# The seven products of an FFN block in another order, with the fourth sum of the weights multiplied last

## The chip, the cores and the metric

The kernel runs on one core of a Trainium2 chip. The metric is the device time of one execution in microseconds (us). The engines are TensorE (PE; PEld is its loading of weights), VectorE (DVE), ScalarE (ACT), GpSimd (POOL) and the sync engine (SP), which issues most DMAs.

## The reference

Two layers of a block with attention, Fourier mixing and a Hyena convolution run over x (512 tokens x 1024) and a context (256 x 1024); each ends with a feed-forward part (FFN). The change is in x's FFN:

```python
def dwconv3(u, w, b):
    up = jnp.pad(u, ((0, 0), (1, 1), (0, 0)))
    return up[:, :-2] * w[0] + up[:, 1:-1] * w[1] + up[:, 2:] * w[2] + b

def conv_ffn(h, w_up, w_c, b_c, w_down):
    u = dwconv3(h @ w_up, w_c, b_c)
    gate, val = jnp.split(u, 2, axis=-1)
    return (jax.nn.silu(gate) * val) @ w_down
```

The hidden width is 2816, so `w_up` is 1024 x 5632 and `w_down` 2816 x 1024. All is float32.

## The kernel before

**Products.** TensorE multiplies float32 values in a reduced form, so every operand is split into a high and a low part and each product is three matmuls: `mm3` does high x high (L196), weight-high x other-low (L197) and weight-low x other-high (L198). `split` makes the parts: ScalarE casts the high part (L181), and VectorE, or GpSimd where it is told so, subtracts it from the source for the low part (L182).

**x's FFN (`ffn_x`).** The hidden width is cut into 22 blocks m of 128 gate and 128 value columns. The up projection of a block, which would be eight products of quarter matrices, is done in the manner of Strassen and Winograd with seven. x's side is cut into quarters by token half and by input half, with sums of quarters S1 to S4 made once. The weights' side is made per block: `prep(m)` loads the raw weights r[0] (gate) and r[1] (value) on the sync queue (L1269, tag "Wm", three buffers), splits r[0] into the quarters "11" and "21", and lets POOL make four differences of quarters: t13 (L1276, L1277) and t24 (L1278, L1279). Each half of t13 gives a factor T1, T3, each half of t24 a factor T2, T4; the "fourth sum" is the second half of t24. The sums' tag "L" has three buffers for two tiles a block. `later()` splits t24, t13 and the second half of r[1] (w22, the quarter "22"), into buffers of the tags "Wh" and "Wl" (four each). In the profile t13 and t24 are both `tt`, their parts `Wh` and `Wl`, w22's parts `w`.

A product is twelve matmuls of a 128 x 128 weight tile with 256 tokens. `first(m)` does 11·11 into the PSUM tile a (copied by ScalarE, L1298) and 12·21 into c (added by VectorE, L1300). `rest(m)` does the other five, in the order 22·T4, S1·T1, S2·T2, S4·22, S3·T3, with a second PSUM tile b; a product with `False` accumulates on what the tile holds. ScalarE copies and VectorE adds collect the results in C0 (gate) and C1 (value). Then the convolution over tokens (L636 to L638, ScalarE and VectorE), silu (ScalarE, L1334), the product gate x value (POOL, L1335) and the split of the result, gT. For blocks after the first, `rest(m)` calls `prep(m + 1)` and `later()` just ahead of the convolution. For block 0, several first products run ahead while norm and modulation are still under way.

**Down projection (`ffn_down`).** Blocks are taken in pairs; the pair before is multiplied with `w_down` (1024 wide, split in the same way) once the present pair's first block is done, and added to y (L1202). So gT is used some two blocks after it is made.

**What sets the order.** The program yields after each product, and a scheduler with a timeline of its own places all instructions: each engine then runs its list strictly in order, and other blocks' products, the down projection's matmuls and the next layer's modulation (for instance the gate's add, L326, which waits for a DMA of `rows`) may come between. PSUM tiles `pn` come from four, `pw` from two buffers.

Of the kernel before, what the change touches and what calls it, by code (L numbers as in the profile page):

```python
# [12 lines left out]
ALU = mybir.AluOpType  # L13
# [55 lines left out]
class Net:  # L69
# [1171 lines left out]
    def ffn_x(self, l):  # L1241

        nc, st = self.nc, self.X
# [9 lines left out]
        def half(a, i):  # L1253
            return a[:, i * 512 : (i + 1) * 512]

        def quad(a, i):
            return a[:, i * 512 : (i + 1) * 512].rearrange("p (k c) -> p k c", c=P)
# [8 lines left out]
        def prep(m):  # L1266
            r = [self.tl([P, 1024], F32, "Wr" if m == 0 else "Wm", "r") for _ in range(2)]
            for e in range(2):
                nc.sync.dma_start(r[e], self.I["w_up"][l, m, e].rearrange("p k c -> p (k c)"))  # L1269
            q = lambda x, i: tuple(quad(a, i) for a in x)  # L1270
            if m not in w:
                h = self.tl([P, 1024], F32R, "Wh"), self.tl([P, 1024], F32R, "Wl")
                self.split(*h, r[0], E0[m] if m < 2 else None)
                w[m] = {"11": q(h, 0), "21": q(h, 1)}
            t13, t24 = (self.tl([P, 1024], F32, "L", "tt") for _ in range(2))
            te.tensor_tensor(half(t13, 0), half(r[1], 0), half(r[0], 0), op=ALU.subtract)  # L1276
            te.tensor_tensor(half(t13, 1), half(r[1], 1), half(r[1], 0), op=ALU.subtract)  # L1277
            te.tensor_tensor(half(t24, 0), half(r[1], 1), half(t13, 0), op=ALU.subtract)  # L1278
            te.tensor_tensor(half(t24, 1), half(t24, 0), half(r[0], 1), op=ALU.subtract)  # L1279

            def later():
                h = [(self.tl([P, 1024], F32R, "Wh"), self.tl([P, 1024], F32R, "Wl")) for _ in range(2)]
                f = self.M("w22")
                with self.tc.issue_after(self.hi) if 0 < m < 3 else self.tc.issue_after(self.mod) if PIN and m == 0 else nullcontext():
                    el = E1[m] if m < 2 else None
                    self.split(*h[1], t24, el)
                    self.split(*h[0], t13, el)
                    self.split(half(f, 0), half(f, 1), half(r[1], 1), el)
                w[m].update({"T1": q(h[0], 0), "T3": q(h[0], 1), "T2": q(h[1], 0), "T4": q(h[1], 1), "22": (quad(f, 0), quad(f, 1))})

            u["w", m] = later
# [11 lines left out]
        def prod(m, ps, left, right, start=True):  # L1303
            for k in range(4):
                wh, wl = w[m][right]
                sh, sl = S[left]
                self.mm3(ps, (wh[:, k], wl[:, k]), (sh[:, k], sl[:, k]), start and k == 0, k == 3, skip_group_check=True)
            yield 12 * C256, 0.0

        def rest(m):  # L1310
            a, C0 = u.pop(m)
            C1 = self.T(512, "C", tag=Z["CT"][2])
            C = C0, C1
            b = self.pn()[:, :256]
            yield from prod(m, b, "22", "T4")
            nc.scalar.copy(C0[:, 256:512], b)
            b = self.pn()[:, :256]
            yield from prod(m, b, "S1", "T1")
            nc.scalar.copy(C1[:, 256:512], b)
            yield from prod(m, a, "S2", "T2", False)  # L1320
            nc.scalar.copy(C1[:, 0:256], a)
            yield from prod(m, b, "S4", "22", False)
            nc.vector.tensor_tensor(C1[:, 0:256], C1[:, 0:256], b, op=ALU.add)
            yield from prod(m, a, "S3", "T3", False)
            nc.vector.tensor_tensor(C0[:, 256:512], a, C0[:, 256:512], op=ALU.subtract)  # L1325
            nc.vector.tensor_tensor(C1[:, 256:512], a, C1[:, 256:512], op=ALU.add)
            if 2 <= m + 1 < MF:
                prep(m + 1)
                u.pop(("w", m + 1))()
            o = [self.T(512, "ft") for _ in range(2)]  # L1330
            for i in range(2):
                self.ffn_conv(l, m, i, o[i], C[i])
            gt = self.M("gT").rearrange("p (e t) -> p e t", e=2)
            nc.scalar.activation(o[0], o[0], AF.Silu)  # L1334
            nc.gpsimd.tensor_tensor(o[0], o[0], o[1], op=ALU.mult)  # L1335
            self.split(gt[:, 0], gt[:, 1], o[0])
            g[m] = gt

        groups = [list(range(a, a + G)) for a in range(0, MF - 4, G)] + [list(range(MF - 4, MF))]
        for i, ms in enumerate(groups):  # L1340
            for j, m in enumerate(ms):
                if m == 0:
                    pw = [self.pw() for _ in range(2)]
                    for n in range(NF[l]):
                        if n < 4:
                            u["a", n] = pw[n % 2][:, n // 2 * 512 : n // 2 * 512 + 512]
                        (prep if n < 2 else prep_first)(n)
                        yield from first(n)
                    if l:
                        self.need("norm_xf3")  # L1350
                    for n in range(2):
                        u.pop(("w", n))()
                    if l == 0 and Z["RC"] == -1:
                        yield from self.rest_c
                    yield from rest(0)
                    if l == 0 and Z["RC"] == 0:
                        yield from self.rest_c
                    continue
                if m >= NF[l]:
                    yield from first(m)  # L1360
                if l == 0 and Z["RC"] == m + 0.5:
                    yield from self.rest_c
                yield from rest(m)
                if l == 0 and Z["RC"] == m:
                    yield from self.rest_c
                if i and j == 0:
                    yield from self.ffn_down(l, st, g, groups[i - 1], i == 1)
# [334 lines left out]
```

## Time and profile before

| | us |
|---|---|
| median of three runs | 1788.12 (1787.71 to 1790.4) |
| profiled execution | 1784.91 |
| its span | 1783.1 |
| TensorE busy | 1639.1 (92%) |
| VectorE busy | 1440.1 (81%) |
| ScalarE busy | 934.9 (52%) |
| GpSimd busy | 692.3 (39%) |

Times within the profile count from the start of the span. x's FFN of layer 0 lies at about 700 to 1070, that of layer 1 at about 1390 to 1765. A row of a timeline gives the start, the duration, the engine, the line, the instruction with out<-in by the program's names, and in brackets how long the engine stood idle ahead of it and which instruction ended that. A row with x2 holds two like instructions in succession.

### The profile page before, as it was taken

To read this page: it belongs to the slowest core of one execution; us is meant where nothing else is said; L and a number is where in the kernel's file an instruction comes from. 1 tells how busy PE (TensorE), PEld (TensorE's weight loads), DVE (VectorE), ACT (ScalarE), POOL (GpSimd) and SP (SyncE) were. 2 spreads that over 40 slices of the span, in tenths; PEclk is the share of its full clock that TensorE was granted. 3 is DMA by queue.
4 is the path that set the end of the run, shared out by engine and by line. 5 is a ranking of instruction groups with operands and counts; after the bars stand their busy time and mean duration, and the time that the engine had idled before them with its cause. 6 is when DMAs were issued, how large, how long until landed. Compare 5 with 4: busy or idle time off the path is not lost. (4 is left out here: it accounts for less than half of the span.)

```text
span 1783.1 us, 27842 instructions
## 1 busy us (share of the span) xinstructions
PE 1639.1 (92%) x10502; PEld 1397.4 (78%) x10502; DVE 1440.1 (81%) x2324; ACT 934.9 (52%) x1737; POOL 692.3 (39%) x515
## 2 busy tenths in 40 slices
PE   5799987899999997989999998998898799999997
PEld 2677775687788897878989885787787678889996
DVE  5888777697665688889988987668895878999997
ACT  2642344487565454556554556434773465555454
POOL 3343332000134337665554645212002455655543
PEclk9899999999999998999999999999999899999999
DMA  9214277603477642332342258653012343332323
GB/s 366 101 61 146 86 243 263 232 13 130 162 253 232 228 155 71 96 118 84 101 148 84 89 185 305 213 175 118 1 48 83 130 146 103 95 107 86 127 62 119
DMA packets 70003, 248.01 MB, mean 139 GB/s; under 512 B 8111, under 2 KB 9647, under 8 KB 69868
## 3 DMA queue, kind: packets, MB, share of 16 engines
q1 hardware_dynamic: 60716, 215.54, 35.6%
q0 software_dynamic: 9152, 30.68, 5.5%
q8 instruction: 83, 1.36, 0.3%
q14 instruction: 52, 0.43, 0.1%
HBM read 232.03 MB, written 14.16 MB: 138 GB/s over the span
## 5 line engine op out<-in xcount | busy, mean ns | idle before, releaser
L196 PE MATMUL pn<-h,Wh 128*128 128x256 f32 x1328 | 376.6, 286 | 11.7 <-DVE ft L638 4.3
L198 PE MATMUL pn<-h,Wl 128*128 128x256 f32 x1328 | 372.8, 284 | 10.2 <-DVE Wl L182 10.2
L197 PE MATMUL pn<-h,Wh 128*128 128x256 f32 x1328 | 374.2, 283 | 1.7 <-POOL h L182 1.7
L196 PEld LDWEIGHTS pn<-h,Wh 128*128 128x128 f32 x1328 | 253.2, 191 | 24.5 <-issue 7.8
L198 PEld LDWEIGHTS pn<-h,Wl 128*128 128x128 f32 x1328 | 252.1, 191 | 15.3 <-DVE Wl L182 12.7
L197 PEld LDWEIGHTS pn<-h,Wh 128*128 128x128 f32 x1328 | 253.8, 191 | 6.2 <-POOL h L182 2.4
L181 ACT CAST Wh<-Wr 128x1024 fp32r<-128x1024 f32 x118 | 122.7, 1049 | 138.9 <-PE pw L198 46.4
L182 DVE TENSOR_TENSOR Wl<-Wr,Wh 128x1024 fp32r<-128x1024 f32 x89 | 129.7, 1465 | 53.7 <-ACT Wh L181 53.2
L1276 POOL TENSOR_TENSOR tt<-r,r 128x512 f32<-128x512 f32 x44 | 75.0, 1705 | 233.9 <-DMA r<-w_up 211.0
L196 PE MATMUL pw<-Wh,gT 128*128 128x512 f32 x352 | 137.5, 404 | 9.0 <-ACT gT L181 3.9
L197 PE MATMUL pw<-Wl,gT 128*128 128x512 f32 x352 | 138.5, 396 | 3.1 <-DVE Wl L182 3.1
L198 PE MATMUL pw<-Wh,gT 128*128 128x512 f32 x352 | 137.8, 396 | 1.8 <-DVE gT L182 1.8
L181 ACT CAST Wh<-tt 128x1024 fp32r<-128x1024 f32 x88 | 90.8, 1048 | 84.9 <-PE pn L197 42.4
L182 DVE TENSOR_TENSOR Wl<-tt,Wh 128x1024 fp32r<-128x1024 f32 x88 | 122.5, 1411 | 11.0 <-ACT Wh L181 8.0
L1335 POOL TENSOR_TENSOR ft<-ft,ft 128x512 f32<-128x512 f32 x44 | 70.8, 1609 | 132.4 <-DVE ft L638 94.2
L1202 DVE TENSOR_TENSOR y<-y,pw 128x1024 f32<-128x1024 f32 x82 | 99.2, 1213 | 20.1 <-PE pw L198 20.0
L182 POOL TENSOR_TENSOR h<-tf,h 128x256 fp32r<-128x256 f32 (+1 forms) x40 | 36.0, 921 | 187.8 <-ACT h L181 186.5
L182 POOL TENSOR_TENSOR Wl<-Wr,Wh 128x1024 fp32r<-128x1024 f32 x29 | 74.6, 2578 | 57.7 <-ACT Wh L181 56.5
L1278 POOL TENSOR_TENSOR tt<-r,tt 128x512 f32<-128x512 f32 x44 | 75.8, 1722 | 51.9 <-DVE Wl L182 51.9
L196 PE MATMUL pw<-h,Wh 128*128 128x256 f32 (+1 forms) x224 | 76.9, 343 | 13.9 <-DVE v L638 2.6
L283 PE MATMUL pn<-wm,cpad 128*32 128x256 f32 x768 | 67.6, 411 | 19.7 <-DMA wm<-w_mod 19.3
L636 ACT ACTIVATE ft<-C,vec 128x512 f32<-128x512 f32 x88 | 68.7, 811 | 32.1 <-DVE C L1325 25.7
(361 smaller groups left out, 4706.1 us busy)
## 6 DMA issues: line engine op xcount, KB each, us to landing
wm<-w_mod SPq DMA_DIRECT2D x96, 512.0 KB, 5.4
r<-w_up SPq DMA_DIRECT2D x90, 512.0 KB, 3.6
Wr<-w_down SPq DMA_DIRECT2D x66, 512.0 KB, 3.8
L<-w_up SPq DMA_DIRECT2D x44, 512.0 KB, 4.4
Wr<-w_out SPq DMA_DIRECT2D x24, 512.0 KB, 3.6
Wr<-w_in_t SPq DMA_DIRECT2D x16, 512.0 KB, 3.9
dft<-hdft_x POOLq DMA_DIRECT2D x16, 512.0 KB, 4.1
Wr<-w_in_c SPq DMA_DIRECT2D x12, 512.0 KB, 3.6
```

What stands on the lines that cost most here:

```text
L181: r = nc.scalar.copy(hi, src)
L182: (el or nc.vector).tensor_tensor(lo, src, f32(hi), op=ALU.subtract)
L196: nc.tensor.matmul(ps, l[0], r[0], start=first, stop=False, **kw)
L197: nc.tensor.matmul(ps, l[0], r[1], start=False, stop=False, **kw)
L198: nc.tensor.matmul(ps, l[1], r[0], start=False, stop=last, **kw)
L283: nc.tensor.matmul(ps[32 * g : 32 * g + 32, cs], self.cpad[:, q % 2 * 4 + g, :], w[:, g, :], start=q % 2 == 0, stop=q % 2 == 1, skip_group ...
L636: nc.scalar.activation(dst, ps, AF.Identity, scale=w1, bias=b)
L1202: nc.vector.tensor_tensor(y, y, acc[t], op=ALU.add)
L1276: te.tensor_tensor(half(t13, 0), half(r[1], 0), half(r[0], 0), op=ALU.subtract)
L1278: te.tensor_tensor(half(t24, 0), half(r[1], 1), half(t13, 0), op=ALU.subtract)
L1335: nc.gpsimd.tensor_tensor(o[0], o[0], o[1], op=ALU.mult)
```

## The change

In `later()` t24 is split last in place of first. In `rest(m)` the five products come in the order S1·T1, S4·22, S2·T2, S3·T3, 22·T4. Before, 22·T4 was copied to C0's second half and subtracted from a at the end; now a is copied there by ScalarE and 22·T4, in a PSUM tile of its own, is subtracted by VectorE as the last step. The number of instructions of each kind is the same: three copies by ScalarE and three adds by VectorE a block.

```diff
                     el = E1[m] if m < 2 else None
-                    self.split(*h[1], t24, el)
                     self.split(*h[0], t13, el)
                     self.split(half(f, 0), half(f, 1), half(r[1], 1), el)
+                    self.split(*h[1], t24, el)
...
             b = self.pn()[:, :256]
-            yield from prod(m, b, "22", "T4")
-            nc.scalar.copy(C0[:, 256:512], b)
-            b = self.pn()[:, :256]
             yield from prod(m, b, "S1", "T1")
             nc.scalar.copy(C1[:, 256:512], b)
+            yield from prod(m, b, "S4", "22", False)
             yield from prod(m, a, "S2", "T2", False)
             nc.scalar.copy(C1[:, 0:256], a)
-            yield from prod(m, b, "S4", "22", False)
             nc.vector.tensor_tensor(C1[:, 0:256], C1[:, 0:256], b, op=ALU.add)
             yield from prod(m, a, "S3", "T3", False)
-            nc.vector.tensor_tensor(C0[:, 256:512], a, C0[:, 256:512], op=ALU.subtract)
+            nc.scalar.copy(C0[:, 256:512], a)
             nc.vector.tensor_tensor(C1[:, 256:512], a, C1[:, 256:512], op=ALU.add)
+            b = self.pn()[:, :256]
+            yield from prod(m, b, "22", "T4")
+            nc.vector.tensor_tensor(C0[:, 256:512], C0[:, 256:512], b, op=ALU.subtract)
```

The new lines of `rest` have the numbers L1316 (copy of S1·T1), L1319 (copy of a after S2·T2), L1320 (add of b), L1322 (copy of a after S3·T3), L1323 (add of a) and L1326 (subtraction of 22·T4).

First, VectorE at the start of layer 0's FFN, as the difference of the two orders. `tt_7139` and `tt_7140` are t13 and t24 of block 0, `tt_7181` and `tt_7182` those of block 1.

```order
+L182 TENSOR_TENSOR Wl_7216<-tt_7139,Wh_7215 128x1024
 L1300 TENSOR_TENSOR C_7145<-C_7145,pn_7146 128x256
 L182 TENSOR_TENSOR Wl_7218<-tt_7140,Wh_7217 128x1024
-L182 TENSOR_TENSOR Wl_7216<-tt_7139,Wh_7215 128x1024
+L182 TENSOR_TENSOR Wl_7227<-tt_7181,Wh_7226 128x1024
 L182 TENSOR_TENSOR gc_7011<-ft_7056,gc_7011 128x256
 L1300 TENSOR_TENSOR C_7187<-C_7187,pn_7188 128x256
 L182 TENSOR_TENSOR Wl_7229<-tt_7182,Wh_7228 128x1024
-L182 TENSOR_TENSOR Wl_7227<-tt_7181,Wh_7226 128x1024
```

The low part of t13 of block 0 moves ahead of block 0's add of 12·21, and that of block 1 ahead of block 1's; ScalarE's casts move in the same way.

Second, VectorE in layer 1 around the gate's add, L326, before. `tt2836` and `tt2837` are t13 and t24 of block 4, `w222842` is its w22, `Wl2857` the low part of block 5's raw gate weights.

```order
L182 TENSOR_TENSOR Wl2835_14907<-r2832_14902,Wh2834_14906 128x1024
L637 SCALAR_TENSOR_TENSOR ft2844_14928<-C2827_14825,vec1_101,ft2844_14928 128x511
L638 SCALAR_TENSOR_TENSOR ft2844_14928<-C2827_14825,vec1_101,ft2844_14928 128x511
L326 TENSOR_TENSOR G2752_14366<-pn2850_14970,bb2849_14968 128x512
L182 TENSOR_TENSOR Wl2841_14919<-tt2837_14911,Wh2840_14918 128x1024
L182 TENSOR_TENSOR Wl2839_14917<-tt2836_14910,Wh2838_14916 128x1024
L182 TENSOR_TENSOR w222842_14920<-r2833_14903,w222842_14920 128x512
L182 TENSOR_TENSOR gT2845_14935<-ft2843_14927,gT2845_14935 128x512
L182 TENSOR_TENSOR Wl2857_15049<-r2854_15044,Wh2856_15048 128x1024
```

And the same place now:

```order
L182 TENSOR_TENSOR Wl2839_14917<-tt2836_14910,Wh2838_14916 128x1024
L637 SCALAR_TENSOR_TENSOR ft2843_14927<-C2738_14304,vec1_101,ft2843_14927 128x511
L637 SCALAR_TENSOR_TENSOR ft2844_14928<-C2827_14825,vec1_101,ft2844_14928 128x511
L638 SCALAR_TENSOR_TENSOR ft2843_14927<-C2738_14304,vec1_101,ft2843_14927 128x511
L638 SCALAR_TENSOR_TENSOR ft2844_14928<-C2827_14825,vec1_101,ft2844_14928 128x511
L1300 TENSOR_TENSOR C2846_14940<-C2846_14940,pn2848_14942 128x256
L326 TENSOR_TENSOR G2752_14366<-pn2850_14970,bb2849_14968 128x512
L182 TENSOR_TENSOR Wl2841_14919<-tt2837_14911,Wh2840_14918 128x1024
L182 TENSOR_TENSOR Wl2857_15049<-r2854_15044,Wh2856_15048 128x1024
L182 TENSOR_TENSOR w222842_14920<-r2833_14903,w222842_14920 128x512
L182 TENSOR_TENSOR gT2845_14935<-ft2843_14927,gT2845_14935 128x512
```

t13's low part has moved ahead of L326, and block 5's first weights ahead of w22 and gT.

Third, TensorE in a block of layer 1's steady part, before. `h2740` and `h2741` are the high and low part of x's quarter 22, `h2743` and `h2744` of S1, `h2745` and `h2746` of S2; `Wh3040` holds T1 and T3, `Wh3042` T2 and T4; `pn3049` is a.

```order
L196 MATMUL pn3052_16336<-h2740_14318,Wh3042_16284 128x256
L197 MATMUL pn3052_16336<-h2741_14319,Wh3042_16284 128x256
L198 MATMUL pn3052_16336<-h2740_14318,Wl3043_16285 128x256
L196 MATMUL pn3053_16350<-h2743_14325,Wh3040_16282 128x256
L197 MATMUL pn3053_16350<-h2744_14326,Wh3040_16282 128x256
L196 MATMUL pn3049_16307<-h2745_14330,Wh3042_16284 128x256
```

And now:

```order
L198 MATMUL pn3052_16336<-h2743_14325,Wl3041_16283 128x256
L196 MATMUL pn3053_16390<-h2740_14318,Wh3042_16284 128x256
L197 MATMUL pn3053_16390<-h2741_14319,Wh3042_16284 128x256
L196 MATMUL pn3049_16307<-h2745_14330,Wh3042_16284 128x256
L197 MATMUL pn3049_16307<-h2746_14331,Wh3042_16284 128x256
L198 MATMUL pn3049_16307<-h2745_14330,Wl3043_16285 128x256
```

Before, the block's five products begin with all of 22·T4, then two matmuls of S1·T1, then S2·T2. Now they begin with S1·T1; two matmuls of 22·T4 and then S2·T2 follow, and the other ten of 22·T4 stand behind S2·T2, ahead of S4·22 and S3·T3.

## Prediction

> **What bounds the kernel now.** I read the page's first part, then the table of windows over the two stretches in which x's feed-forward part runs, then TensorE's timeline for the waits inside them, and last the engines that those waits name. The profiled execution took 1784.91 us (span 1783.1); the median of the three runs is 1788.12, 3.2 more, and I carry that difference along unchanged. About 0.2%, 3.6 us, is what a measurement of this kernel can tell from no change.
>
> The first line is the page's busy line; the others are windows (length, then busy time of PE, PEld, DVE, ACT, POOL, the granted clock, the DMA share and GB/s).
>
> ```profile
> PE 1639.1 (92%) x10502; PEld 1397.4 (78%) x10502; DVE 1440.1 (81%) x2324; ACT 934.9 (52%) x1737; POOL 692.3 (39%) x515
> 700.00:910.00 210.00, 193.95 (x1300) 177.95 (x1299) 183.74 (x230) 117.81 (x189) 121.45 (x72) 0.96 0.34 110
> 910.00:1060.00 150.00, 146.43 (x1020) 135.20 (x1020) 134.38 (x150) 78.25 (x123) 77.09 (x50) 1.00 0.34 110
> 1395.00:1492.00 97.00, 81.65 (x582) 71.08 (x581) 79.72 (x94) 49.43 (x79) 56.35 (x36) 0.93 0.40 132
> 1492.00:1755.00 263.00, 259.49 (x1784) 239.16 (x1784) 243.60 (x271) 139.11 (x216) 129.48 (x78) 1.00 0.32 102
> ```
>
> TensorE sets the pace. In the steady part of layer 1 it is busy for 259.49 of 263 us and in layer 0 for 146.43 of 150: 3.5 us in each is all that any order of work could win there, and the number of products is unchanged. In the ramps, where the first blocks' weights are still being made, it is idle for 16 of 210 and 15 of 97 us. VectorE is next: 243.60 of 263 is 93%, so in the steady part it has little to give. A gain has to come from the ramps and a loss would come through VectorE.
>
> These are TensorE's waits in the ramps that the change can reach (start, duration, instruction, and in brackets the idle time ahead of it with its releaser):
>
> ```profile
> 722.85 0.39 PE L196 MATMUL pn<-h,Wh 128*128 128x256 f32 x1 [0.31 <-ACT Wh L181]
> 724.11 0.39 PE L198 MATMUL pn<-h,Wl 128*128 128x256 f32 x1 [0.75 <-DVE Wl L182]
> ...
> 732.72 0.28 PE L198 MATMUL pn<-h,Wl 128*128 128x256 f32 x1
> ...
> 733.77 0.28 PE L198 MATMUL pn<-h,Wl 128*128 128x256 f32 x1
> 736.05 0.39 PE L196 MATMUL pn<-h,w 128*128 128x256 f32 x1 [2.00 <-ACT C L1319]
> ...
> 764.99 0.38 PE L196 MATMUL pn<-h,Wh 128*128 128x256 f32 x1 [0.62 <-ACT Wh L181]
> 766.49 0.39 PE L198 MATMUL pn<-h,Wl 128*128 128x256 f32 x1 [1.00 <-DVE Wl L182]
> ...
> 1472.74 0.38 PE L198 MATMUL pn<-h,Wl 128*128 128x256 f32 x1 [1.06 <-DVE Wl L182]
> 1474.98 0.38 PE L198 MATMUL pn<-h,Wl 128*128 128x256 f32 x1 [0.55 <-DVE Wl L182]
> 1480.57 0.58 PE L198 MATMUL pn<-h,Wl 128*128 128x256 f32 x1 [2.51 <-DVE Wl L182]
> ```
>
> In layer 0 they make 0.31 + 0.75 + 2.00 + 0.62 + 1.00 = 4.68 us, in layer 1 1.06 + 0.55 + 2.51 = 4.12 us. From 732.72 to 733.77 nine matmuls start in 1.05 us, 0.117 each, so a product of twelve is 1.4 us.
>
> **Part 1: the split of t13 ahead of that of t24, layer 0.** The rows are of ScalarE, VectorE, GpSimd (POOL) and the sync queue, in order of time:
>
> ```profile
> 705.76 0.37 ACT L1298 COPY C<-pw 128x256 f32<-128x256 f32 x1 [8.27 <-PE pw L198]
> 706.17 0.42 DVE L1300 TENSOR_TENSOR C<-C,pn 128x256 f32<-128x256 f32 x1 [2.29 <-ACT C L1298]
> 707.11 2.36 DVE L182 TENSOR_TENSOR Wl<-tt,Wh 128x1024 fp32r<-128x1024 f32 x2 [0.53 <-ACT Wh L181]
> 708.42 2.21 POOL L1278 TENSOR_TENSOR tt<-r,tt 128x512 f32<-128x512 f32 x1 [4.99 <-DVE Wl L182]
> 710.65 1.76 SPq L1269 DMA_DIRECT2D r<-w_up  x2
> 714.08 1.46 POOL L1276 TENSOR_TENSOR tt<-r,r 128x512 f32<-128x512 f32 x1 [2.02 <-DMA r<-w_up]
> 720.10 1.61 POOL L1279 TENSOR_TENSOR tt<-tt,r 128x512 f32<-128x512 f32 x1
> 721.75 2.00 ACT L181 CAST Wh<-tt 128x1024 fp32r<-128x1024 f32 x2 [3.68 <-POOL tt L1279]
> ```
>
> There are three buffers for the sums. Block 1's t24 (708.42) waits 4.99 us for the first of the two splits at 707.11 to free one. Only when it has read the raw weights does the sync queue load block 2's (710.65); POOL then waits for them (714.08), ends block 2's fourth sum at 721.71, and ScalarE has sat 3.68 us for that sum, with the cast of t13, whose sums were ready, queued behind. In the new order the cast of t13 of block 0 stands ahead of the copy at 705.76, into ScalarE's 8.27 us of idleness, and its lo part ahead of the add at 706.17, into VectorE's 2.29 us from 703.88. One lo part is 2.36 / 2 = 1.18 us, so a buffer is free at about 705.1 in place of 708.3: 3.2 us earlier. The load, its DMA and the sums of block 2 follow by the same 3.2 us (nothing else stands between 703.4 and 708.4 on POOL), and the cast of t13 no longer waits for the fourth sum at all. TensorE's waits of 0.31 and 0.75 are shorter than 3.2 and go. The wait of 2.00 hangs on POOL too:
>
> ```profile
> 730.91 1.29 POOL L1335 TENSOR_TENSOR ft<-ft,ft 128x512 f32<-128x512 f32 x1
> 732.23 0.62 ACT L181 CAST gT<-ft 128x512 fp32r<-128x512 f32 x1 [5.23 <-POOL ft L1335]
> 735.64 0.36 ACT L1319 COPY C<-pn 128x256 f32<-128x256 f32 x1
> ```
>
> The copy at 735.64 frees the bank that TensorE wants; it is late because the cast of gT ahead of it waited 5.23 us for the product at 730.91, which stood behind a sum of block 3. With the sums 3.2 us earlier the product runs earlier too, and 2.00 goes. The pair at 764.99 and 766.49 (1.62) is a t13 cast that arrived late on ScalarE; it now stands earlier there and I count it as gone. Together −4.68 us; if only the first two waits go, −1.1.
>
> **Part 2: the same in layer 1.** VectorE's timeline:
>
> ```profile
> 1470.86 0.69 DVE L326 TENSOR_TENSOR G<-pn,bb 128x512 f32<-128x512 f32 x1 [5.15 <-DMA bb<-rows]
> 1471.47 3.45 DVE L182 TENSOR_TENSOR Wl<-tt,Wh 128x1024 fp32r<-128x1024 f32 x2
> 1474.85 1.77 DVE L182 TENSOR_TENSOR w<-r,w 128x512 fp32r<-128x512 f32 x1
> ...
> 1478.23 2.28 DVE L182 TENSOR_TENSOR Wl<-r,Wh 128x1024 fp32r<-128x1024 f32 x1
> ```
>
> A gate operation (L326) holds VectorE for 5.15 us on a DMA, and both lo parts of block 4, its w22, gT and the next block's first weights (1478.23) wait behind it. In the new order t13's lo part stands ahead of L326 and the next block's first weights two rows behind it, ahead of w22 and gT, as the order in the section on the change shows. So T1's lo part is there before the wait, and the first weights are done at about 1471.5 + 1.7 (half of 3.45) + 2.3 = 1475.5 in place of 1480.5, which is more than the 2.51 us that TensorE waits for them. −4.12 us; a gain under 2 if t24's lo part, still behind L326, is then the one waited for.
>
> **Part 3: the products and copies.** Three ScalarE copies and three VectorE adds a block stay, of the same shapes (0.36 and 0.42 us above); no matmul and no DMA comes or goes. Two things are new. A bank must now be copied out between S1·T1 and S4·22, and between S2·T2 and S3·T3, where in the scheduled order other products mostly lie between; at block 10 of layer 0 next to nothing does. What one uncovered read of a bank costs is in the steady part:
>
> ```profile
> 1585.36 0.39 PE L196 MATMUL pn<-h,Wh 128*128 128x256 f32 x1 [0.69 <-DVE C L1323]
> ```
>
> Two of these make +1.4 us. And at a block's end the add into C1 waits for the copy of the same bank (L1322): in this trace both readers were VectorE's, one after the other. VectorE stands still for up to 0.36 us, with the third add, the convolutions and the next lo parts behind it. Two blocks pass before gT is used, which covers it; where gT is already late, at the two waits below, it would add 0.36 each. The Trainium skill (PSUM — Partial Sum Buffer, "PSUM bank collisions raise a hardware error") says two engines must not touch one bank at once, reads against reads included, so copy and add can't overlap; by that rule, with all 44 blocks paying the copy's 0.36 on the path, the sum would be 16 us worse. No row here shows a reader held up in that way.
>
> ```profile
> 1555.25 0.50 PE L196 MATMUL pw<-Wh,gT 128*128 128x512 f32 x1 [0.80 <-ACT gT L181]
> 1559.10 0.50 PE L198 MATMUL pw<-Wh,gT 128*128 128x512 f32 x1 [0.88 <-DVE gT L182]
> ```
>
> These 1.68 us may go (gT of these blocks stands some us earlier in VectorE's new order); I set them, with 0.6 more of small change, against what VectorE's tighter order costs in the steady part.
>
> **A cost of moving POOL's sums.** Two lo parts take 2.36 us with POOL idle and 3.46 beside POOL's sums:
>
> ```profile
> 713.17 3.46 DVE L182 TENSOR_TENSOR Wl<-tt,Wh 128x1024 fp32r<-128x1024 f32 x2 [1.93 <-ACT Wh L181]
> ...
> 722.83 2.36 DVE L182 TENSOR_TENSOR Wl<-tt,Wh 128x1024 fp32r<-128x1024 f32 x2 [0.23 <-ACT Wh L181]
> ```
> ```profile
> 725.31 1.69 POOL L1276 TENSOR_TENSOR tt<-r,r 128x512 f32<-128x512 f32 x1 [3.60 <-DVE Wl L182]
> ```
>
> Block 1's t24, moved to 705.1, now lies beside the splits at 707.11, 1.1 us of extra VectorE time, and the same may happen once more; VectorE's 1.93 us of idleness ahead of 713.17 covers it. The Trainium skill (SBUF — State Buffer, "Who interferes with whom") has the rule: a VectorE instruction with both inputs in SBUF shares its second read port with GpSimd's reads. The trace agrees; by the rule, without that cover, the sum would be 2.2 us worse.
>
> **The sum.** −4.68 − 4.12 + 1.4 = −7.4, with −0.6 for the balance of gT and the steady part: −8. From the profile's own 1784.9 to 1776.9, and the median to **1780**. The likeliest case's own range is 1776 to 1784.
>
> **The rivals.**
> *Slower: t24's lo part comes too late.* Before, the first product of the five needs t24's lo part and the one that needs t13's follows 24 matmuls on. Now the first needs t13's, and S2·T2 needs t24's 14 matmuls on: 10 x 0.117 = 1.2 us sooner, with w22's 1.77 us put ahead of it on VectorE. Its lead shrinks by 2.9 us in every block. That decides as soon as VectorE is less than 2.9 us ahead of TensorE, and it is 93% busy. Where each pair of blocks also brings two w_down splits it could bite: 11 of 44 blocks at half of 2.9 is +16 us, less the 8: 1796. Against it: no wait for a Wl stands in the steady part of layer 1 now, so VectorE is ahead there. Chance 0.2.
> *No change: the gain is handed back.* TensorE gets 4.7 us ahead in layer 0 and then meets w_down parts from VectorE which are not earlier:
>
> ```profile
> 784.55 0.50 PE L197 MATMUL pw<-Wl,gT 128*128 128x512 f32 x1 [1.97 <-DVE Wl L182]
> 791.59 0.50 PE L197 MATMUL pw<-Wl,gT 128*128 128x512 f32 x1 [1.11 <-DVE Wl L182]
> ...
> 896.55 0.50 PE L196 MATMUL pw<-Wh,gT 128*128 128x512 f32 x1 [2.20 <-ACT Wh L181]
> ```
>
> Then these waits grow by what was won, and layer 1 keeps about 2 of its 4 us, less the 1.4: 1787.5. For it: they come right after the ramp. Against it: VectorE's work of the ramp is earlier too, by its filled holes (2.29, 1.93). Chance 0.22.
> *More:* the three waits just shown (5.28) go as well: 1775. Chance 0.1.
> *The change doesn't do what it says:* the scheduler orders the products itself, and in many blocks 22·T4 stands between S1·T1 and S2·T2, not last. Then the copy at the block's end is no longer hurried or delayed by it and only the splits matter; part 3's 1.4 falls away, and the time is 1779, inside the forecast.
>
> **How the numbers follow.** Forecast 0.48, more 0.1, no change 0.22, slower 0.2. The range leaves out the far half of the slower case and little else: 1771 to 1793. Faster by over 0.2% (below 1784.5): 0.48 + 0.1 = 0.58; the same 0.22; slower 0.2.
>
> **What would show it.** Right: POOL's L1278 of block 1 at about 705, the third load of raw weights at about 707.5, no wait at the products after 722; no wait of 2.5 us behind L326. Wrong: new waits `pn L198 <- DVE Wl` in 1492 to 1755, or the waits at 784 and 791 grown to 4 us and more. A steady part that is longer by more than 3 us would make the slower rival right.

## The result, and the profile after

The changed kernel took 1817.5 us (median of four runs) beside 1788.8 for the kernel before: a ratio of 1.0156, interval 1.0139 to 1.0173, 28.6 us slower. The profiled execution's span is 1817.3 us. It took 1.6 us more than its kernel's median, and the profiled execution of before 3.9 less than its own, so the two profiles lie 34.2 us apart; the stretches and waits below are of these two.

The busy line of the page after, and windows over the stretches that were shown of before, moved by the delay so far:

```profile
PE 1650.5 (91%) x10502; PEld 1405.3 (77%) x10502; DVE 1428.9 (79%) x2324; ACT 935.3 (51%) x1737; POOL 695.9 (38%) x515
700.00:910.00 210.00, 185.20 (x1254) 168.52 (x1253) 180.66 (x221) 114.02 (x183) 119.45 (x70) 0.98 0.33 106
917.00:1067.00 150.00, 143.10 (x985) 132.28 (x984) 127.58 (x143) 76.42 (x119) 81.09 (x48) 0.99 0.33 104
1409.00:1506.00 97.00, 79.40 (x555) 69.43 (x554) 74.34 (x91) 45.70 (x73) 52.25 (x33) 0.89 0.40 131
1506.00:1769.00 263.00, 251.88 (x1685) 229.81 (x1684) 220.00 (x252) 131.59 (x205) 131.95 (x80) 0.99 0.30 90
```

TensorE has the same 10502 matmuls, is busy for 11.4 us more (1650.5 beside 1639.1) and idle for 22.8 more (span less busy time: 166.8 beside 144.0). In the steady part it was idle for 3.5 of 263 us and is for 11.1; VectorE's busy time there fell from 243.60 to 220.00.

The rows of TensorE's waits from 700 to 1800 that name a copy or an add which reads a PSUM tile (C), each with the total, the number and the longest; first those of before, where two smaller rows add 0.7, then the four largest of after, where two more add 2.1:

```profile
PE pn L196 <- ACT C L1319: 2.0, 1, 2.0
PE pn L196 <- DVE C L1323: 1.7, 4, 0.7
PE pw L196 <- ACT C L1321: 1.4, 1, 1.4
```
```profile
PE pn L196 <- ACT C L1298: 8.3, 7, 2.0
PE pn L196 <- ACT C L1316: 6.6, 3, 5.5
PE pn L196 <- DVE C L1320: 3.8, 2, 3.3
PE pn L196 <- DVE C L1323: 3.4, 3, 1.1
```

In all 5.8 us before and 24.2 after: 18.4 of the 22.8 us. These matmuls may not start until a tile has been read out, since they accumulate on it (behind L1298, L1316) or take its buffer (L1320, L1323).

The starts of the adds to y (L1202) divide the time: from the 18th to the 50th of them (layer 0's FFN) it is 339.5 us before and 351.1 after; from the 59th to the last (five pairs of blocks of layer 1) 168.5 and 182.4; from the 31st add of the residual (L1113) to the 51st add to y (layer 1's ramp) 106.7 and 112.0. So +11.6, +13.9 and +5.3 us; what lies ahead of layer 0's FFN moved by 1.7, the stretch between the two FFNs by 0.1, the one between the ramp and the five pairs by -1.6, and what follows the last add by 3.3. Not all of the 13.9 is lost there: by the windows further down 1178 matmuls lie in that stretch and 1145 before, and 28 more at 0.118 us and 5 more at 0.231 (the usual times from start to start before) are 4.5 us of it.

Of the signs that the prediction named for being right, the sum, the load and the missing wait behind L326 came; that no wait is left at the products after 722 didn't. These are rows of POOL, the sync queue, TensorE and VectorE of the profile after (this execution was 1.7 us later at the start of layer 0's FFN):

```profile
706.87 1.29 POOL L1278 TENSOR_TENSOR tt<-r,tt 128x512 f32<-128x512 f32 x1 [1.72 <-DVE Wl L182]
708.19 2.56 SPq L1269 DMA_DIRECT2D r<-w_up  x2
728.68 0.39 PE L198 MATMUL pn<-h,Wl 128*128 128x256 f32 x1 [2.62 <-DVE Wl L182]
1488.24 0.69 DVE L326 TENSOR_TENSOR G<-pn,bb 128x512 f32<-128x512 f32 x1
```

Less 1.7, the sum starts at 705.2, as forecast, and the load at 706.5 (about 707.5 was forecast), and L326 holds up nothing: no idle time is noted ahead of it. But in place of the three waits of 3.06 us from 722 to 736 stands a new one of 2.62, and one of 0.91 at 733.90; and of the pair at 764.99 and 766.49, counted as gone, 1.11 us is left, at 765.06.

The largest new wait of a ramp is in layer 1. TensorE's row, then ScalarE's ahead of it:

```profile
1459.49 0.58 PE L196 MATMUL pn<-h,w 128*128 128x256 f32 x1 [5.46 <-ACT C L1316]
```
```profile
1456.63 0.62 ACT L181 CAST gT<-ft 128x512 fp32r<-128x512 f32 x1 [2.15 <-POOL ft L1335]
1457.15 0.61 ACT L181 CAST w<-r 128x512 fp32r<-128x512 f32 x1
1457.67 1.51 ACT L636 ACTIVATE ft<-C,vec 128x512 f32<-128x512 f32 x2
1459.09 0.35 ACT L1316 COPY C<-pn 128x256 f32<-128x256 f32 x1
```

S4·22 may not accumulate until S1·T1 has been copied out. The copy takes 0.35 us, but it stands behind a cast that waits for POOL, another cast and two convolutions.

In the steady part, TensorE's waits of before (1562 to 1730) and after (1579 to 1761), each with the total, the number and the longest:

```profile
PE pn L196 <- DVE C L1323: 1.1, 3, 0.7
PE pw L196 <- DVE y L1202: 0.7, 2, 0.4
```
```profile
PE pn L196 <- ACT C L1298: 2.6, 2, 1.3
PE pn L198 <- DVE Wl L182: 2.3, 5, 0.7
PE pw L196 <- ACT Wh L181: 1.2, 3, 0.4
PE pn L196 <- ACT C L1319: 0.7, 3, 0.2
```

The lists differ by 5.0 us only. Measured from start to start, against 0.118 and 0.231 us, matmuls that begin over 0.15 us late make 8.9 us after and 2.6 before in these stretches, and smaller delays 3.9 and 0.9, of which some 1.5 us belong to one spell at half the clock (shown at the end). One of the first line's two, TensorE and then ScalarE:

```profile
1628.39 0.39 PE L196 MATMUL pn<-h,Wh 128*128 128x256 f32 x1 [1.33 <-ACT C L1298]
1629.62 0.39 PE L198 MATMUL pn<-h,Wl 128*128 128x256 f32 x1 [0.73 <-DVE Wl L182]
```
```profile
1626.50 0.63 ACT L1334 ACTIVATE ft<-ft 128x512 f32<-128x512 f32 x1 [2.27 <-DVE ft L638]
1627.04 1.03 ACT L181 CAST Wh<-r 128x1024 fp32r<-128x1024 f32 x1
1627.97 0.36 ACT L1298 COPY C<-pn 128x256 f32<-128x256 f32 x1
```

S2·T2's first matmul waits for the copy of 11·11, which stands behind a cast and a silu (L1334) that waits for VectorE; its third waits for t24's low part. The first chain was not among the rivals; the second was.

### The profile page after: what moved, and what is told of

Same layout as the page of the kernel before. It is cut to its first block, busy times and chain, and to the rows that moved or that the text cites. A ratio compares the mean times of both kernels' runs of the same rounds, so it can differ in the third digit from the quotient of the medians.

```text
span 1817.3 us, 27854 instructions
## 1 busy us (share of the span) xinstructions
PE 1650.5 (91%) x10502; PEld 1405.3 (77%) x10502; DVE 1428.9 (79%) x2324; ACT 935.3 (51%) x1737; POOL 695.9 (38%) x515
## 5 line engine op out<-in xcount | busy, mean ns | idle before, releaser
L196 PE MATMUL pn<-h,Wh 128*128 128x256 f32 x1328 | 382.2, 289 | 27.1 <-ACT C L1298 8.3
L198 PE MATMUL pn<-h,Wl 128*128 128x256 f32 x1328 | 375.0, 286 | 13.6 <-DVE Wl L182 13.5
L197 PE MATMUL pn<-h,Wh 128*128 128x256 f32 x1328 | 376.6, 284 | 0.0
L198 PEld LDWEIGHTS pn<-h,Wl 128*128 128x128 f32 x1328 | 253.6, 193 | 19.4 <-DVE Wl L182 18.0
L182 DVE TENSOR_TENSOR Wl<-Wr,Wh 128x1024 fp32r<-128x1024 f32 x89 | 121.3, 1366 | 70.9 <-ACT Wh L181 61.4
L182 DVE TENSOR_TENSOR Wl<-tt,Wh 128x1024 fp32r<-128x1024 f32 x88 | 126.6, 1446 | 18.4 <-ACT Wh L181 18.4
L198 PE MATMUL pw<-Wh,gT 128*128 128x512 f32 x352 | 138.7, 397 | 0.8 <-DVE gT L182 0.7
L1202 DVE TENSOR_TENSOR y<-y,pw 128x1024 f32<-128x1024 f32 x82 | 99.3, 1214 | 35.9 <-PE pw L198 35.5
L637 DVE SCALAR_TENSOR_TENSOR ft<-C,vec,ft 128x511 f32<-128x511 f32 x88 | 84.5, 998 | 1.8 <-ACT ft L636 1.8
```

The lines of the kernel that those rows point to most:

```text
L182: (el or nc.vector).tensor_tensor(lo, src, f32(hi), op=ALU.subtract)
L196: nc.tensor.matmul(ps, l[0], r[0], start=first, stop=False, **kw)
L197: nc.tensor.matmul(ps, l[0], r[1], start=False, stop=False, **kw)
L198: nc.tensor.matmul(ps, l[1], r[0], start=False, stop=last, **kw)
L637: nc.vector.scalar_tensor_tensor(dst[:, 1:T], ps[:, 0 : T - 1], w0, dst[:, 1:T], op0=ALU.mult, op1=ALU.add)
L1202: nc.vector.tensor_tensor(y, y, acc[t], op=ALU.add)
```

## The experiments

Three theories were there at the start. A: t24's low part is late (the prediction's slower rival). B: the new order ties convolution, silu and the copies of a into one chain on ScalarE. C: the edit makes the scheduler lay the FFN out anew, and the layout, not the edit, costs the time. D came later: a layout's cost is VectorE's backlog. All ratios are to the kernel before on the same chip. Where nothing is said of pinning, the scheduler drew the order anew for the edit.

**The two halves of the change apart.** Splits alone, in the kernel before:

```diff
-                    self.split(*h[1], t24, el)
                     self.split(*h[0], t13, el)
                     self.split(half(f, 0), half(f, 1), half(r[1], 1), el)
+                    self.split(*h[1], t24, el)
```

> The kernel before with the order of the splits alone (t13, w22, t24). Theory A (the low part of t24 comes too late): the five products still begin with 22·T4, which needs it, so this is the worst mixture: over 1800 us, with waits for Wl ahead of 22·T4. Theory B (the products' new order, with gate and value both finished at the block's very end, puts the convolution, silu and the copies of a behind each other): products and copies are those of before, so within 5 us of 1788. Theory C (any edit makes the scheduler lay out the FFN anew, and most layouts are worse): somewhere between 1795 and 1820.

1818.0 us, ratio 1.0158 (1.0132 to 1.0183). B, within 5 us of 1788, missed; the time suits A and C. But what A names isn't there: from 700 to 1800 TensorE waits for `pn L198 <- DVE Wl` 4.8 us in six places, before 7.2 in eight. The longest row is of gT:

```profile
PE pw L198 <- DVE gT L182: 22.6, 13, 2.2
```

Products and copies alone, in the changed kernel:

```diff
+                    self.split(*h[1], t24, el)
                     self.split(*h[0], t13, el)
                     self.split(half(f, 0), half(f, 1), half(r[1], 1), el)
-                    self.split(*h[1], t24, el)
```

> The changed kernel with the splits in the order of before (t24, t13, w22); products and copies as changed. Theory A: the waits of S2·T2's third matmul for t24's low part go (10 us in all with the slow stretch of TensorE behind them), 1800 or less. Theory B: the waits of S2·T2's first matmul for the copy of a stay, 1810 to 1820. Theory C: between 1795 and 1820, no rule.

1812.9 us, 1.0130 (1.0100 to 1.0160). A, 1800 or less, missed: with t24 split first, 24 us of the loss stay. B's and C's ranges both hold the time. Each half costs nearly as much as the whole: they don't add up, which speaks for C.

**t24 second.**

```diff
                     self.split(*h[0], t13, el)
-                    self.split(half(f, 0), half(f, 1), half(r[1], 1), el)
                     self.split(*h[1], t24, el)
+                    self.split(half(f, 0), half(f, 1), half(r[1], 1), el)
```

> The changed kernel with t24 split second, ahead of w22, instead of last; TensorE's order is nearly that of the changed kernel. Theory A: t24's low part is ready 0.7 to 1.8 us sooner, which is more than the waits of 0.4 to 0.9 us at S2·T2's third matmul, so they go: 1807 to 1811. Theory B: those waits were in the shadow of the copy, and the time stays at 1815 to 1819.

1820.8 us, 1.0176 (1.0153 to 1.0199). One of its waits in the steady part:

```profile
PE pn L198 <- DVE Wl L182: 2.3, 5, 0.7
```

The wait for the low part is the same 2.3 us in five places. But this doesn't speak against A: in these five pairs VectorE, ScalarE and GpSimd run the same lines on the same tiles in the same order as in the changed kernel (175, 139 and 54 instructions), so the scheduler didn't carry the edit out there. What weighs against A as the cause of the whole loss is the run before.

**A neutral edit.**

```diff
-            nc.vector.tensor_tensor(C0[:, 256:512], a, C0[:, 256:512], op=ALU.subtract)
             nc.vector.tensor_tensor(C1[:, 256:512], a, C1[:, 256:512], op=ALU.add)
+            nc.vector.tensor_tensor(C0[:, 256:512], a, C0[:, 256:512], op=ALU.subtract)
```

> The kernel before with its last two adds, L1325 and L1326, in the other order: no dependence, count or duration changes. Theories A and B: 1786 to 1791. Theory C: the scheduler's layout of the FFN changes with any edit, and the time moves by over 5 us, mostly up.

1808.5 us, 1.0104 (1.0083 to 1.0126): 20 us for two adds that changed places. From here on some kernels have their order pinned: at the end of the program each engine's instructions are tied, one behind the other, to the order that they have in a kernel named (`names` is that list of one engine). Such a tie waits for nothing.

```diff
+def _pin(tc):
...
+        for x, y in zip(names, names[1:]):
+            tc.add_manual_dep(bb[y], x, info, reason="pin")
...
         Net(tc, I, out, (sb, psw, psn, dr)).run()
+        _pin(tc)
```

**The same swap, pinned to the old order.**

> The kernel before with L1325 and L1326 swapped, as in the last run, but with every engine's order of instructions pinned to that of the kernel before, so that the two adds change places and nothing else moves. Theory C (the layout costs the time, not the edit): 1785 to 1791. If the swap of the adds costs the 20 us itself: 1803 to 1810.

1788.2 us, 0.9992 (0.9979 to 1.0005). So the swap costs nothing; the layout that the scheduler drew for it cost the 20 us. This is shown.

**The old products in the changed kernel's layout.**

> The kernel before (its own products, copies and splits), with all instructions outside the five products, their six copies and adds and the three splits pinned to the order that they have among themselves in the changed kernel; the scheduler places the block's own. Theory C: 1805 to 1820, most of the 28 us without the change. Theories A and B: near the kernel before, 1785 to 1795.

1821.8 us, 1.0164 (1.0132 to 1.0196). The kernel before loses all that the changed one loses, without the change, once everything around the block's own work is laid out as for the change; the block's own products, copies, adds and splits were left to the scheduler, so this is a mixture and not the layout alone.

**Silu behind the copy.** An edge from each block's silu to the next block's L1298:

```diff
+                i, j = (getattr(x, "ins", x) for x in (EDGE[l, m, "silu"], EDGE[l, m + 1, "copy"]))
+                tc.add_manual_dep(i, j.name, info, reason="silu behind the copy")
```

> The changed kernel with one rule more for the scheduler: on ScalarE the silu of a block stands behind the next block's copy of a (L1298). Theory B (S2·T2 waits for that copy, which stands behind a silu that waits for the convolution): the waits ahead of S2·T2's first matmul go, 14 us in both layers with some of the slow stretches behind them, and the time is 1798 to 1808. If the wait only moves to the next thing VectorE is late with: 1813 to 1820.

1819.7 us, 1.0167 (1.0146 to 1.0189). The waits in the steady part, for the same stretch as above:

```profile
PE pn L198 <- DVE Wl L182: 3.2, 3, 1.7
PE pw L196 <- ACT gT L181: 3.1, 3, 1.0
```

The wait for L1298 is gone here and TensorE waits as long for low parts and for gT, as the second expectation said. B named a wait, and without it the time is no lower. As the order was drawn anew, this doesn't price the wait by itself.

**gT's low part on GpSimd**, in the kernel before, pinned:

```diff
-            self.split(gt[:, 0], gt[:, 1], o[0])
+            self.split(gt[:, 0], gt[:, 1], o[0], P_)
```

> The kernel before with the low part of gT made by GpSimd in place of VectorE (44 x 0.68 = 30 us off VectorE), every other instruction pinned to its place. Theory D (VectorE's backlog is what TensorE's waits in any layout come from): the waits shrink and it runs 3 to 10 us faster, 1778 to 1785. If only the order counts: 1788, and slower, to 1795, where gT comes late since GpSimd needs twice as long.

1799.8 us, 1.0053 (1.0035 to 1.0071), slower:

```profile
PE pw L198 <- POOL gT L182: 8.5, 7, 2.0
PE pw L196 <- ACT gT L181: 6.5, 5, 2.5
```

11 us lost, and TensorE now waits for gT's parts. That is slower than either forecast. But it is no test of D, since VectorE was hardly relieved. Its busy time is that of before, 1440.1 us (1447.9 in the pinned swap), with 44 instructions fewer:

```profile
PE 1642.3 (91%) x10502; PEld 1395.4 (78%) x10502; DVE 1440.1 (80%) x2280; ACT 934.5 (52%) x1737; POOL 757.6 (42%) x559
```

The 44 subtractions had taken 43.9 us; others got longer while GpSimd was busier, the 88 L637 of 128 x 511 from 81.3 to 94.2 us in all, those of w22 from 48.2 to 54.8.

**The changed products in the old layout.**

> The changed kernel (its products, copies and splits) in the layout of before: every instruction of layer 1 and of the rest outside a block's own five products, copies, adds and splits keeps the order that it has in the kernel before; in layer 0's FFN the first two products with their copy and add, and ScalarE's casts, are left to the scheduler, since all of it together can't be placed. Theory C (the layout costs the 28 us, the change itself nothing): 1785 to 1795. If the change's own order of products costs: 1805 or more.

1821.5 us, 1.0180 (1.0148 to 1.0212). C as I had put it (the change itself costs nothing) missed, and the other forecast, 1805 or more if the change's own order costs, holds. Here too the block's own work was left to the scheduler, a mixture the other way round. In layer 1's steady part the waits have mostly one place, with VectorE's row of what holds it up:

```profile
1678.53 0.47 PE L196 MATMUL pw<-Wh,gT 128*128 128x512 f32 x1 [3.14 <-DVE y L1202]
```
```profile
1673.97 0.42 DVE L1320 TENSOR_TENSOR C<-C,pn 128x256 f32<-128x256 f32 x1 [5.45 <-PE pn L198]
```

VectorE stands for 5.45 us in front of the add of S4·22's result, and an add to y that frees a PSUM tile is queued behind. In layer 0 the old order can't be kept whole, since instructions of the changed kernel would wait for each other in a circle; so how it does wholly in the old layout wasn't tried.

**w22's low part left out**, in both kernels, each in its own layout. The subtraction does 8 of 512 columns, and S4·22 takes the high part in the low part's place, so the output is not the reference's:

```diff
-                    self.split(half(f, 0), half(f, 1), half(r[1], 1), el)
+                    nc.scalar.copy(half(f, 0), half(r[1], 1)); (el or V_).tensor_tensor(half(f, 1)[:, 0:8], r[1][:, 512:520], f32(half(f, 0)[:, 0:8]), op=ALU.subtract)
...
-                w[m].update({"T1": q(h[0], 0), "T3": q(h[0], 1), "T2": q(h[1], 0), "T4": q(h[1], 1), "22": (quad(f, 0), quad(f, 1))})
+                w[m].update({"T1": q(h[0], 0), "T3": q(h[0], 1), "T2": q(h[1], 0), "T4": q(h[1], 1), "22": (quad(f, 0), quad(f, 0))})
```

> The changed kernel in its own layout, pinned, with w22's low part left out: the subtraction does 8 of 512 columns, and S4·22 takes the high part in its place, so VectorE has some 40 us less to do (44 x 1.1 less a rest) and TensorE the same. Theory D (what a layout costs are TensorE's waits for work that VectorE is late with): 1795 to 1803. If the waits are fixed chains that a free VectorE doesn't shorten: 1810 to 1817.

> The same left out of the kernel before, in its own pinned layout. Theory D: TensorE is busy for 98 to 99% of the steady part already, so only the ramps gain: 1781 to 1786, much less than in the changed kernel's layout. If VectorE is the bound: 1770 or less.

1805.6 us, 1.0106 (1.0068 to 1.0144), and 1776.1 us, 0.9930 (0.9908 to 0.9952). The subtractions took 25 us less in each, not 40, since one of 8 columns still takes 0.4 to 0.5 us; VectorE's busy time fell by 23 (to 1405.6 and 1417.2). This gives 12 and 14 us. Within the intervals that is the same in both. It is more than I expected of the kernel before, and in the changed kernel lies between the two forecasts. The 29 us between the layouts stay. D explains a part of the time in either, not the difference.

**The neutral edits in both kernels.** The swap in the changed kernel (its add ahead of its copy of a), POOL's two halves of t13 in the other order, and the two loads in the other order:

```diff
-            nc.scalar.copy(C0[:, 256:512], a)
             nc.vector.tensor_tensor(C1[:, 256:512], a, C1[:, 256:512], op=ALU.add)
+            nc.scalar.copy(C0[:, 256:512], a)
```
```diff
-            te.tensor_tensor(half(t13, 0), half(r[1], 0), half(r[0], 0), op=ALU.subtract)
             te.tensor_tensor(half(t13, 1), half(r[1], 1), half(r[1], 0), op=ALU.subtract)
+            te.tensor_tensor(half(t13, 0), half(r[1], 0), half(r[0], 0), op=ALU.subtract)
```
```diff
-            for e in range(2):
+            for e in (1, 0):
                 nc.sync.dma_start(r[e], self.I["w_up"][l, m, e].rearrange("p k c -> p (k c)"))
```

> The changed kernel with its copy and add after S3·T3 (L1322, L1323) in the other order; nothing is pinned. Theory C: the scheduler lays the FFN out anew and the time moves by 5 us or more in either direction, between 1800 and 1830. Otherwise 1815 to 1820.

> A second neutral edit of the kernel before, nothing pinned: POOL makes the two halves of t13 in the other order (they don't depend on each other). Theory C' (the kernel before is an unusually good layout, and any redrawing costs some 20 us): 1800 to 1815. If the swap of the adds was only bad luck: 1785 to 1793.

> The same edit in the changed kernel. Theory C': anywhere from 1800 to 1825, on average no more than 10 us above the redrawn kernels before. If the new order of products has a cost of its own of 20 us or more: 1825 or more, since the redrawn kernel before lies at about 1805.

> A third neutral edit of the kernel before: the two loads of raw weights of a block are issued in the other order. Theory C': 1800 to 1815. Otherwise 1785 to 1793.

> The same edit in the changed kernel. Theory C': 1800 to 1825, with the mean of the three redrawn changed kernels within 10 us of that of the three redrawn kernels before. A cost of the new order itself: a difference of the means of 20 us or more.

| | before, us (ratio) | changed, us (ratio) | five pairs of layer 1, us |
|---|---|---|---|
| as written | 1788.8 | 1817.5 (1.0156) | 168.5; 182.4 |
| adds or add and copy swapped | 1808.5 (1.0104) | 1807.2 (1.0103) | 176.3; 167.5 |
| halves of t13 swapped | 1801.1 (1.0075) | 1858.3 (1.0392) | 167.5; 199.3 |
| loads swapped | 1821.0 (1.0190) | 1829.2 (1.0241) | 187.5; 189.0 |

Every redrawn kernel before is slower, by 12 to 32 us. The changed kernel's 28.6 lies within that span. That it is the draw and not the edit is shown for the swap alone, which was also pinned; for the halves and the loads, which can also change when data are there, it is argued. Layer 0's FFN (339.5 us before) takes 346.3 to 355.0 in the three redrawn before and 351.5 to 360.2 in the three redrawn changed. The means of the three redrawn are 1810 and 1832; they differ by 21 us, but without one kernel (1858) it would be 8, two of the three pairs are within 9 us, and the spread in a column is 20 and 51 us. My test took a difference of the means of 20 as a sign of a cost of its own, and 10 as the most that C' allows, so by its letter it came out for a cost of the new order; with such a spread I don't hold the time for settled.

The traces do tell the two kinds of kernel apart. TensorE's waits for a tile to be read out (the rows that name the tile C, as above, from 690 us on) make 4.2 to 9.4 us in the ten kernels with the old products in an order that was drawn for old products, and 12.9 to 30.6 in all nine with the changed ones, in whatever order; the old products in the changed layout have 16.3. They don't give the time by themselves: 9.4 goes with 1821.0 and 12.9 with 1807.2, where other waits are longer or shorter.

The last column shows that the changed products can do layer 1's five pairs in 167.5 us, as before's 168.5. Windows over these five pairs, of before, of after and of the changed kernel with the swap:

```profile
1562.00:1730.60 168.60, 166.80 (x1145) 153.79 (x1144) 158.40 (x173) 89.87 (x138) 89.22 (x55) 1.00 0.31 98
```
```profile
1579.00:1761.40 182.40, 175.65 (x1178) 160.20 (x1177) 153.13 (x175) 89.36 (x139) 91.64 (x55) 0.99 0.29 90
```
```profile
1576.80:1744.30 167.50, 166.32 (x1130) 151.75 (x1129) 152.55 (x170) 85.78 (x134) 85.31 (x53) 1.00 0.32 98
```

**w22's low part on GpSimd**, in the kernel before, pinned:

```diff
-                    self.split(half(f, 0), half(f, 1), half(r[1], 1), el)
+                    self.split(half(f, 0), half(f, 1), half(r[1], 1), P_)
```

> The kernel before in its own pinned layout, with the low part of w22 (needed only by S4·22, late in a block) made by GpSimd in place of VectorE. With that part left out the same layout took 1776. If what it gains is VectorE's time: 1778 to 1785, faster than both kernels. If GpSimd's later sums and gate-value products give it back, as with gT: 1788 to 1800.

1789.5 us, 1.0007 (0.9993 to 1.0021): no gain. Here too VectorE's busy time stayed (1441.8 us, with 44 instructions fewer). No version that computes everything beat the kernel before.

**The new wait by itself**, in the kernel before, pinned: a copy of a that nobody reads, ahead of the two adds.

```diff
-            yield from prod(m, a, "S3", "T3", False)
+            yield from prod(m, a, "S3", "T3", False); nc.scalar.copy(JK[0], a[:, 0:56])
             nc.vector.tensor_tensor(C0[:, 256:512], a, C0[:, 256:512], op=ALU.subtract)
```

> The kernel before in its own pinned layout, with one more ScalarE copy a block, of 56 columns of a after S3·T3 into a tile that nobody reads; VectorE's add L1325, which reads the same bank, now waits for it, as the changed kernel's L1323 waits for its copy. This prices that wait alone, which the prediction took as hidden. If it is hidden: 1786 to 1791. If it is on a path that sets the pace (44 waits of 0.3 us and what queues behind them): 1800 or more, a good part of the 28 us.

1795.6 us, 1.0037 (1.0021 to 1.0053): 6.6 us by the ratio, between the two forecasts. The line's page shows the wait, and that of the changed kernel's L1323 shows none:

```profile
L1325 DVE TENSOR_TENSOR C<-pn,C x38: 406/423/427, 740.4 to 1753.8; 128x256 f32<-128x256 f32 x38
...
its engine sat idle before it (us, times) until:
  ACT jk L1324: 25.0, 20
```
```profile
L1323 DVE TENSOR_TENSOR C<-pn,C x38: 409/411/418, 741.0 to 1783.6; 128x256 f32<-128x256 f32 x38
...
its engine sat idle before it (us, times) until:
who waited for it (us, times):
```

Put into an order that wasn't drawn for it, the wait idles VectorE for 25 us and costs 6.6. In the changed kernel's own order VectorE never idles there. So VectorE's wait for the copy is not what the 28 us are.

## Why the prediction was wrong

*What held.* TensorE as the bound; the earlier sums and load (705.2 and 706.5); L326 no longer in the way, and with it 3 of layer 1's 4.12 us of waits for low parts (1.0 is left from 1406 to 1506); the new wait of VectorE for ScalarE's copy hidden, as forecast.

*The step that failed is the sum itself*, by a term that it lacks, the new order, and by one that it has far too small, the bank read below. It took the waits of the trace before, crossed out those whose named cause moved (4.68 and 4.12 us), and left every other row standing. But the order is drawn anew, in both FFNs and to their ends. Some of the waits went and others came: 2.62 us at 728.68 for 3.06 in layer 0, and in the end 11.6 us more for its FFN. The swap of two adds pinned to the old order changes nothing and unpinned costs 20 us; with the two other small edits it is 12 to 32. That cost wasn't among the terms, nor among the rivals; "the scheduler orders the products itself" stood there as a matter of 1.4 us.

*"The steady part: plus or minus nothing".* I set gT's 1.68 us and 0.6 more against VectorE's tighter order. The steady part of layer 1 alone gave +13.9 us.

*The uncovered bank read, +1.4 us*, is the term that was mis-sized most. The mechanism was right, but it was counted twice at 0.69 us, from a row in which the add came 0.7 us after TensorE was ready for it. The trace after has 24.2 us of such waits for 5.8: 18.4 in place of 1.4. At 1459.49 one was 5.46 us, since the 0.35 us copy stood in ScalarE's queue behind a cast that waited for POOL; and the largest group, 8.3 us ahead of S2·T2 (L1298), part 3 didn't name. They lie in both layers (10.6 us in layer 0's FFN, 7.4 in layer 1's ramp), not at block 10 alone. How much of this is the new products and how much the order drawn for them isn't separated.

*The slower rival* had the right sign and nearly the right place (the third matmul of S2·T2 does wait, 2.3 us in the five pairs), but isn't the cause of the whole: the waits are 2.3 of the 13.9 us there, and with t24 split first (products and copies alone) the kernel is still at 1812.9.

*The rule on shared banks* (16 us worse by it, if on the path): the trace after doesn't show it on the path; with a shorter copy (56 columns, 0.20 us) in an order not drawn for it, it is 6.6 us.

*What stays open:* how much of the 28.6 us the new order of products costs by itself; the waits for tiles speak for a part, the times don't settle it. The mixed kernels (old products in the new layout, new products in most of the old) both took 1821 to 1822 us, so a layout suits the products it was drawn for and neither half can be blamed alone. What makes the layout of the kernel before so much better than its neighbours wasn't found: neither one wait (ScalarE's copy, t24) nor VectorE's load explains it alone.

## What to carry to other kernels

Where a scheduler places the instructions, an edit is two things: the edit, and a new draw of the order. Before costing the first from a trace, price the second with an edit that changes no dependence; here such edits cost 0.7 to 1.9%, several times what a measurement can tell. Pinning shows what an edit is worth where the old order suits it, as with the swap; it can't where the edit changes the order itself. See in the trace that an edit was carried out, and that an engine meant to be relieved is less busy, before a run is read as a test of either. And price a wait by what stands ahead of the awaited instruction in its own engine's queue, not by that instruction's duration.

## What the runs showed of the hardware

A spell of half the clock followed two short waits of TensorE, once out of twice. The pair of waits shown at 1628 comes again 66 us on; here its rows, and then windows of the profile after, the first behind the earlier pair:

```profile
1694.77 0.39 PE L196 MATMUL pn<-h,Wh 128*128 128x256 f32 x1 [1.23 <-ACT C L1298]
...
1696.01 0.40 PE L198 MATMUL pn<-h,Wl 128*128 128x256 f32 x1 [0.73 <-DVE Wl L182]
```
```profile
1630.00:1635.00 5.00, 5.00 (x45) 5.00 (x44) 4.51 (x6) 2.02 (x4) 0.68 (x1) 1.00 0.52 132
1693.00:1696.00 3.00, 1.05 (x7) 0.63 (x5) 3.00 (x4) 3.00 (x5) 1.28 (x1) 1.00 0.00 0
1696.00:1698.00 2.00, 1.99 (x13) 1.99 (x14) 2.00 (x3) 1.24 (x4) 0.00 (x0) 0.76 0.00 0
1698.00:1700.00 2.00, 2.00 (x11) 2.00 (x11) 1.76 (x3) 0.45 (x2) 0.00 (x0) 0.50 0.87 256
```

After the first pair the granted clock stayed at 1.00. After the second it fell to 0.50: in the 2 us from 1698 nine matmuls begin, one in 0.21 us, where 17 would at 0.117 each. (The counts in the windows take in every matmul that reaches into them.) The Trainium skill (TensorE: Matmul & The Clock Gate, "What's actually happening") has the clock fall after an idle window of about 3.4 us that runs freely; here the fall came behind 1.96 us of waiting within 2.5, and none behind 2.06 within 2.6. That the waits brought it on is not shown.

Work handed from VectorE to GpSimd hardly came off VectorE in these runs. With 44 subtractions of 128 x 512 made by GpSimd, GpSimd's busy time rose from 692.3 us to 757.6 (gT) and 758.8 (w22), and VectorE's was 1440.1 and 1441.8, beside 1440.1 before and 1447.9 in the pinned swap: at most 8 us came off, of some 44 and 48.
